# The last two casting loads of a Winograd convolution, each cut into two halves of 32 rows

## The chip, the cores and the metric

The kernel runs on one core of a Trainium2 chip. The metric is device time in microseconds (us), the median of the runs. The engines are named as in the profile: PE (TensorE: matmuls; PEld: its weight loads), DVE (VectorE), ACT (ScalarE), POOL (GpSimd) and SP (SyncE, which here only issues DMAs). All DMAs of the core run on 16 DMA engines.

## The reference

A 3x3 convolution with padding 1 over 16 images, 64 channels in, 128 out, 64x64 pixels, all in float32:

```python
batch, c_in, h, w, c_out = 16, 64, 64, 64, 128
x_pad = np.pad(x, ((0, 0), (0, 0), (1, 1), (1, 1)), mode='constant')
output = np.zeros((batch, c_out, h, w), dtype=np.float32)
for b in range(batch):
    for co in range(c_out):
        for ci in range(c_in):
            for kh in range(3):
                for kw in range(3):
                    output[b, co] += weight[co, ci, kh, kw] * x_pad[b, ci, kh:kh+h, kw:kw+w]
```

## The kernel before

The images are worked on in eight pairs `p`; two images of 64 channels fill the 128 partitions. A pair's input is one tile `xs[p]` of 64x64 float16 on each partition. The pool `xpool` has eight buffers, one for each pair, so no load waits for a buffer.

**How the input comes in.** Pairs 0 to 2 are loaded by SP as float32 (`x0`, `x1`, `x2`) and cast by ACT and POOL in pieces of 14 to 18 rows (L97 and L98). Pairs 3 to 7 are loaded by POOL with a DMA that casts from float32 to float16 on the way (`load`, L56 to L58), one DMA of 64 rows for a pair: 2 MB are read and 1 MB is written. POOL issues pairs 3 and 4 behind its casts of pair 0 (L107), and pairs 5, 6 and 7 one behind the other in pair 1's turn of the main loop (L132 to L134). No other DMA stands in POOL's queue.

**The scheme.** It is a Winograd form along the rows: two output rows 2j and 2j+1 share one product with the sum of the input rows 2j and 2j+1. `sums` (L62 to L67) forms these row sums `ss[p]`, for pair 0 on DVE and for all others on POOL, in two instructions of 16 sums (32 input rows) each, `lo` = 0 and 16. The pool `spool` has three buffers. The combined weights (`Wt`: G0, G21, G1, G01, G2) are made once at the start.

**The main loop** (L128) runs over the pairs. POOL first forms the sums of the next pair (L130, L131). Then come four blocks of 8 row pairs. A block has three groups of matmuls (L168): `U` from `ss` (6 matmuls), then `A` and `Bt` from `xs` (12 each, in pairs for the two images). ACT copies `U` out of PSUM (L182), DVE adds it to `A` (L190) and to `Bt` (L193) into the output tile `ot`. The rows of `xs` that a block reads follow from an offset: block 1 (sums 8 to 15) reads rows 15 to 31, and its last six matmuls (G2, offset 2) rows 18 to 32.

**The stores.** The first image of a pair is stored by SP, the second by ACT, each as one DMA of 2 MB, in halves of 1 MB for pair 7 and for the first image of pair 0. ACT's store is held back and issued in the next block's turn (L184). The output tiles have seven buffers, three of which first hold `x0` to `x2`.

**The order.** `keep` (L28) holds the marked instructions of one engine in the order in which the program has them: POOL's casts, sums and loads, ACT's copies and casts, ACT's stores. The framework sets the semaphores: each of POOL's DMAs reports its landing, and whoever reads the rows that it writes waits for that.

The lines of the change in their place:

Of the kernel before, what the change touches and what calls it, by code (L numbers as in the profile page):

```python
# [13 lines left out]
def kernel(  # L14
# [6 lines left out]
    nc = tc.nc  # L21
    B, CI, H, W = x.shape
# [5 lines left out]
    keep = tc.keep_in_program_order  # L28
    x_rows = x.rearrange("b c h w -> (b c) h w")
# [23 lines left out]

    xs = {p: xpool.tile([128, H, W], F16, tag="xs", name="xs") for p in range(3)}

    def load(p):  # L56
        xs[p] = xpool.tile([128, H, W], F16, tag="xs", name="xs")
        keep(nc.gpsimd.dma_start(xs[p], x_rows[128 * p : 128 * p + 128, :, :]))  # L58

    ss = {}  # L60

    def sums(eng, p, src, lo, n):  # L62
        if p not in ss:
            ss[p] = spool.tile([128, H // 2, W], F16, tag="ss", name="ss")
        v = src.rearrange("p (j i) c -> p j i c", i=2)
        keep(
            eng.tensor_add(  # L67
                ss[p][:, lo : lo + n, :], v[:, lo : lo + n, 0, :], v[:, lo : lo + n, 1, :]
            )
        )  # L70
# [26 lines left out]
    def cast(copy, p, src, lo, hi):  # L97
        keep(copy(xs[p][:, lo:hi, :], src[:, lo:hi, :]))  # L98
# [6 lines left out]
    cast(nc.gpsimd.tensor_copy, 0, x0, 34, 50)  # L105
    cast(nc.gpsimd.tensor_copy, 0, x0, 50, 64)
    for p in (3, 4):  # L107
        load(p)
    later = {
        (0, 0): [(0, x0, 18, 34)],  # L110
        (0, 2): [(1, x1, 0, 16), (1, x1, 16, 32)],
# [10 lines left out]
    def store(eng, p, b2, ot, lo, hi):  # L122
        return eng.dma_start(
            out_rows[2 * p + b2, :, lo:hi, :],
            ot.rearrange("p j i c -> p (j i) c")[:, lo:hi, :],
        )

    for p in range(NP):  # L128
        if p + 1 < NP:
            for lo in (0, 16):  # L130
                sums(nc.gpsimd, p + 1, raws.get(p + 1, xs[p + 1]), lo, 16)  # L131
                if (p, lo) == (1, 16):  # L132
                    for q in range(5, NP):
                        load(q)  # L134
        ots = [
            opool.tile([128, H // 2, 2, W], F32, tag="ot", name="ot") for _ in range(2)
        ]
        for blk in range(4):
            j0 = blk * RB

            def group(wi_rows):

                tiles = [
                    psum.tile([128, RB, W], F32, tag="acc", name="acc") for _ in range(2)
                ]
                n = 3 * len(wi_rows)
                i = 0
                for wi, off in wi_rows:
                    for kw in (1, 0, 2):
                        c_lo, c_hi = max(0, 1 - kw), min(W, W + 1 - kw)  # L150
                        for b2 in range(2):
                            p0 = 64 * b2
                            lo, hi = j0, j0 + RB
                            if off is None:
                                rhs = ss[p][p0 : p0 + 64, lo:hi, c_lo + kw - 1 : c_hi + kw - 1]
                            else:
                                while 2 * lo + off < 0:
                                    lo += 1
                                while 2 * (hi - 1) + off > H - 1:
                                    hi -= 1  # L160
                                first = 2 * lo + off
                                last = 2 * (hi - 1) + off
                                rhs = xs[p][
                                    p0 : p0 + 64,
                                    first : last + 1 : 2,
                                    c_lo + kw - 1 : c_hi + kw - 1,
                                ]
                            nc.tensor.matmul(  # L168
                                tiles[b2][:, lo - j0 : hi - j0, c_lo:c_hi],
                                Wt[p0 : p0 + 64, wi, kw, :],  # L170
                                rhs,
                                start=i == 0,
                                stop=i == n - 1,
                            )
                        i += 1
                return tiles

            U = group([(G1, None)])
            us = []
            for b2 in range(2):  # L180
                ut = upool.tile([128, RB, W], F32, tag="ut", name="ut")
                keep(nc.scalar.copy(ut, U[b2]))  # L182
                us.append(ut)
            while held and (p, blk) != (1, 0):  # L184
                keep(store(nc.scalar, *held.pop(0)))
            for piece in later.get((p, blk), ()):
                cast(nc.scalar.copy, *piece)
            A = group([(G21, 1), (G0, -1)])
            for b2 in range(2):
                nc.vector.tensor_add(ots[b2][:, j0 : j0 + RB, 0, :], A[b2], us[b2])  # L190
            Bt = group([(G01, 0), (G2, 2)])
            for b2 in range(2):
                nc.vector.tensor_add(ots[b2][:, j0 : j0 + RB, 1, :], Bt[b2], us[b2])  # L193
            if blk in cuts_of[p][0]:
                store(nc.sync, p, 0, ots[0], *cuts_of[p][0][blk])
            if blk in cuts_of[p][1]:
                held.append((p, 1, ots[1], *cuts_of[p][1][blk]))
# [32 lines left out]
```

## Time and profile before

| | us |
|---|---|
| median of 3 runs | 126.29 (126.21 to 126.46) |
| profiled execution, its own time | 126.58 |
| profiled execution, span from first to last instruction | 124.8 |
| PE busy | 107.6 (86%) |
| DVE busy | 84.5 (68%) |
| ACT busy | 46.5 (37%) |
| POOL busy | 37.5 (30%) |

The mean granted clock of PE is 0.971 of full speed, and is lower only in the last slices, when PE has ended. HBM is read for 17.07 MB and written with 33.55 MB by the instructions' account. The DMA part of the page counts a packet by the bytes that it writes, so a casting load of 2 MB in float32 shows as 1 MB. In that part q0 is POOL's queue, q1 SP's, q10 ACT's; q8 and q14 fetch instructions. The time of a queue is the sum of its packets' times as a share of 16 engines' span.

### The profile page before, as it was taken

To read this page: it belongs to the slowest core of one execution; us is meant where nothing else is said; L and a number is where in the kernel's file an instruction comes from. 1 tells how busy PE (TensorE), PEld (TensorE's weight loads), DVE (VectorE), ACT (ScalarE), POOL (GpSimd) and SP (SyncE) were. 2 spreads that over 40 slices of the span, in tenths; PEclk is the share of its full clock that TensorE was granted. 3 is DMA by queue.
4 is the path that set the end of the run, shared out by engine and by line. 5 is a ranking of instruction groups with operands and counts; after the bars stand their busy time and mean duration, and the time that the engine had idled before them with its cause. 6 is when DMAs were issued, how large, how long until landed. Compare 5 with 4: busy or idle time off the path is not lost.

```text
span 124.8 us, 2427 instructions
## 1 busy us (share of the span) xinstructions
PE 107.6 (86%) x984; PEld 50.2 (40%) x984; DVE 84.5 (68%) x135; ACT 46.5 (37%) x78; POOL 37.5 (30%) x28
## 2 busy tenths in 40 slices
PE   0598999999999999999999999999999999991000
PEld 0543444444444444444444444444444444440000
DVE  1009987878877887877777778777877787775000
ACT  4108649966663333333333333333333333330000
POOL 2209790899594003900066000930000000000000
PEclk9999999999999999999999999999999999999855
DMA  5999999999999999999999999999999999999991
GB/s 131 394 431 452 441 302 229 284 284 289 365 349 336 341 381 349 365 344 336 373 362 365 334 347 415 441 436 420 415 447 415 436 410 441 431 402 418 425 407 53
DMA packets 4042, 45.52 MB, mean 365 GB/s; under 512 B 448, under 2 KB 448, under 8 KB 576
## 3 DMA queue, kind: packets, MB, share of 16 engines
q1 hardware_dynamic: 2016, 23.36, 45.0%
q10 hardware_dynamic: 1296, 16.78, 31.7%
q0 software_dynamic: 720, 5.24, 20.5%
q8 instruction: 7, 0.11, 0.3%
q14 instruction: 3, 0.02, 0.0%
HBM read 17.07 MB, written 33.55 MB: 406 GB/s over the span
## 4 chain that ended last, share of the span: by engine, by line
PE 81%; DMA 6%; DVE 2%; issue 1%; DVEq 0%; SPq 0%
PE acc L168 81%; DMA x<-in_x_dram 6%; DVE ot L190 1%; DVE ss L67 1%; DVE ot L193 0%; DVEq L225 0%; SPq L41 0%; DVEq L190 0%
## 5 line engine op out<-in xcount | busy, mean ns | idle before, releaser
L168 PE MATMUL acc<-xs,Wt 64*128 64x504 f16 (+3 forms) x768 | 87.2, 373 | 0.0
L168 PEld LDWEIGHTS <-Wt 64*128 64x128 f16 x960 | 47.3, 94 | 56.2 <-issue 1.1
L182 ACT COPY ut<-acc 128x512 f32<-128x512 f32 x64 | 34.4, 589 | 56.9 <-issue 39.0
L190 DVE TENSOR_TENSOR ot<-acc,ut 128x512 f32<-128x512 f32 x64 | 41.2, 685 | 20.8 <-PE acc L168 18.4
L193 DVE TENSOR_TENSOR ot<-acc,ut 128x512 f32<-128x512 f32 x64 | 41.1, 683 | 0.0
L67 POOL TENSOR_TENSOR ss<-xs 128x1024 f16<-128x1024 f16 x10 | 21.1, 2127 | 32.6 <-DMA xs<-in_x_dram 20.5
L168 PE MATMUL acc<-ss,Wt 64*128 64x504 f16 (+1 forms) x192 | 26.1, 377 | 0.6 <-DVE ss L67 0.6
L98 ACT CAST xs<-x 128x1024 f16<-128x1024 f32 (+1 forms) x10 | 10.5, 1070 | 3.5 <-DMA x<-in_x_dram 3.5
L67 POOL TENSOR_TENSOR ss<-x 128x1024 f16<-128x1024 f32 x4 | 9.4, 2365 | 4.3 <-DMA x<-in_x_dram 4.3
L67 DVE TENSOR_TENSOR ss<-x 128x512 f16<-128x512 f32 x4 | 3.3, 867 | 7.8 <-DMA x<-in_x_dram 7.8
L85 PE MATMUL wp<-ident,w 128*64 128x128 f16 x18 | 1.3, 328 | 4.4 <-POOL w L52 4.4
L98 POOL CAST xs<-x 128x1024 f16<-128x1024 f32 (+1 forms) x2 | 3.0, 1519 | 4.7 <-DMA x<-in_x_dram 4.7
L91 PE MATMUL warm<-blank 128*128 128x400 f32 x6 | 3.6, 757 | 0.0
L85 PEld LDWEIGHTS <-w 128*64 128x64 f16 x18 | 1.1, 210 | 4.4 <-POOL w L52 4.4
L58 POOL DMA_DIRECT2D xs<-in_x_dram x5 | 2.9, 579 | 0.0
L91 PEld LDWEIGHTS warm<-blank 128*128 128x128 f32 x6 | 1.7, 304 | 1.4 <-issue 1.2
L92 ACT CAST Wt<-wp 128x384 f16<-128x384 f32 x1 | 0.5, 479 | 3.1 <-PE wp L85 3.1
L92 ACT ACT_TABLE_LOAD x1 | 1.3, 1283 | 0.7 <-PEq L214 0.7
L52 POOL CAST w<-w_raw 128x576 f16<-128x576 f32 x1 | 0.7, 662 | 2.4 <-DMA w_raw<-in_weight_dram 2.4
L88 DVE MEMSET blank<- 128x400 f32 x1 | 0.4, 392 | 0.9 <-PEq L214 0.9
L103 ACT CAST Wt<-wp 128x384 f16<-128x384 f32 x1 | 0.5, 478 | 0.5 <-DVE Wt L95 0.5
L94 DVE TENSOR_TENSOR Wt<-wp,Wt 128x384 f16<-128x384 f32 x1 | 0.6, 550 | 0.0
(8 smaller groups left out, 1.9 us busy)
## 6 DMA issues: line engine op xcount, KB each, us to landing
out_dram<-ot ACTq DMA_DIRECT2D x7, 2048.0 KB, 19.4
out_dram<-ot SPq DMA_DIRECT2D x6, 2048.0 KB, 19.1
x<-in_x_dram SPq DMA_DIRECT2D x3, 2048.0 KB, 12.3
xs<-in_x_dram POOLq DMA_DIRECT2D x5, 1024.0 KB, 21.7
out_dram<-ot SPq DMA_DIRECT2D x4, 1024.0 KB, 11.8
out_dram<-ot ACTq DMA_DIRECT2D x2, 1024.0 KB, 10.9
w_raw<-in_weight_dram SPq DMA_DIRECT2D x1, 288.0 KB, 2.9
```

The costliest lines, as they stand in the source:

```text
L52: keep(nc.gpsimd.tensor_copy(w16, w_raw))
L58: keep(nc.gpsimd.dma_start(xs[p], x_rows[128 * p : 128 * p + 128, :, :]))
L67: eng.tensor_add(ss[p][:, lo : lo + n, :], v[:, lo : lo + n, 0, :], v[:, lo : lo + n, 1, :])
L85: nc.tensor.matmul(wp[q : q + 64, k * CO : k * CO + CO], w16[:, t::9], ident)
L91: nc.tensor.matmul(warm[:, 0:400], blank[:, 0:128], blank)
L92: keep(nc.scalar.copy(wrow(G1), wps[1]))
L94: keep(nc.vector.tensor_sub(wrow(G21), wps[2], wrow(G1)))
L98: keep(copy(xs[p][:, lo:hi, :], src[:, lo:hi, :]))
L168: nc.tensor.matmul(tiles[b2][:, lo - j0 : hi - j0, c_lo:c_hi], Wt[p0 : p0 + 64, wi, kw, :], rhs, start=i == 0, stop=i == n - 1,)
L182: keep(nc.scalar.copy(ut, U[b2]))
L190: nc.vector.tensor_add(ots[b2][:, j0 : j0 + RB, 0, :], A[b2], us[b2])
L193: nc.vector.tensor_add(ots[b2][:, j0 : j0 + RB, 1, :], Bt[b2], us[b2])
```

## The change

`load` takes a number of rows and issues one DMA for each such part of the tile. Pairs 3, 4 and 5 come in one DMA of 64 rows as before; pairs 6 and 7 in two DMAs of 32 rows, one behind the other in POOL's queue. A half reads 8 KB that lie together from each of 128 channel planes (before: 16 KB) and writes 4 KB to each partition. POOL issues seven casting DMAs instead of five. Nothing else is edited.

```diff
-    def load(p):
+    def load(p, rows):
         xs[p] = xpool.tile([128, H, W], F16, tag="xs", name="xs")
-        keep(nc.gpsimd.dma_start(xs[p], x_rows[128 * p : 128 * p + 128, :, :]))
+        for lo in range(0, H, rows):
+            keep(
+                nc.gpsimd.dma_start(
+                    xs[p][:, lo : lo + rows, :],
+                    x_rows[128 * p : 128 * p + 128, lo : lo + rows, :],
+                )
+            )
...
     for p in (3, 4):
-        load(p)
+        load(p, H)
...
                 if (p, lo) == (1, 16):
                     for q in range(5, NP):
-                        load(q)
+                        load(q, H if q == 5 else H // 2)
```

## The prediction

> **What bounds the kernel now.** I read the page first: the engines' shares, the DMA row of the 40 slices, the queues and the chain.
>
> ```profile
> span 124.8 us, 2427 instructions
> PE 107.6 (86%) x984; PEld 50.2 (40%) x984; DVE 84.5 (68%) x135; ACT 46.5 (37%) x78; POOL 37.5 (30%) x28
> ...
> DMA  5999999999999999999999999999999999999991
> ...
> q1 hardware_dynamic: 2016, 23.36, 45.0%
> q10 hardware_dynamic: 1296, 16.78, 31.7%
> q0 software_dynamic: 720, 5.24, 20.5%
> ...
> PE 81%; DMA 6%; DVE 2%; issue 1%; DVEq 0%; SPq 0%
> ```
>
> At first sight this is a TensorE kernel: PE is the longest engine and carries 81% of the chain. But the chain follows instructions, and its last is the issue of a store near 114 us; the 11 us behind it, to 124.8, are transfers. And the DMA row shows 9 in every slice from the second to the last but one. The three data queues add up: 45.0 + 31.7 + 20.5 = 97.2% of the time of 16 DMA engines. q1 is SP's queue (the early plain loads and half of the stores), q10 ACT's (the other stores), q0 GpSimd's casting loads. Next I looked for gaps, in the table of stretches (columns: stretch, length, busy time of PE, PEld, DVE, ACT and POOL with their counts, clock, DMA share, GB/s):
>
> ```profile
> 40.00:55.00 15.00, 15.00 (x144) 6.91 (x140) 11.51 (x19) 5.03 (x10) 4.21 (x2) 1.00 1.01 354
> 78.00:100.00 22.00, 22.00 (x208) 10.17 (x206) 17.06 (x29) 7.52 (x14) 4.20 (x2) 1.00 1.01 432
> 100.00:112.00 12.00, 12.00 (x116) 5.53 (x112) 9.23 (x15) 4.29 (x8) 0.00 (x0) 1.00 1.00 419
> 112.00:122.50 10.50, 0.61 (x8) 0.10 (x2) 1.98 (x4) 0.00 (x0) 0.00 (x0) 0.76 0.93 393
> ```
>
> PE is full to 112, and the DMA share is 1.00 or 1.01 up to there too, with stores still to be drained. (The lower GB/s of 40 to 55 is bookkeeping: a casting load is counted by the bytes it writes, half of those it reads.) So two bounds run side by side, and the transfers end last. How far behind is PE's own path? The last two stores, one row of the timeline and one of the DMA view for 113 to 115, and the page's row of a small load (size, and us from issue to landing):
>
> ```profile
> 114.01 0.34 ACTq L123 DMA_DIRECT2D out_dram<-ot  x1
> ```
> ```profile
> out_dram<-ot SPq DMA_DIRECT2D x1, 1024.0 KB, 9.8
> ```
> ```profile
> w_raw<-in_weight_dram SPq DMA_DIRECT2D x1, 288.0 KB, 2.9
> ```
>
> The two last stores are 2 MB together: at the 393 GB/s of the last stretch 5.3 us. They land after 9.8, so 4.5 us are latency and waiting behind older stores. The small load bounds the latency: 288 KB at 432 GB/s are 0.7 us, so 2.2 of its 2.9 us are fixed. That leaves 2.3 us by which PE's last pair could be late before the end of the kernel moved. The end therefore moves by what the change adds to the work of the DMA engines, one for one, and by a late load only beyond that slack.
>
> **What the change adds for the DMA engines.** The counts in the page say how a transfer is cut. q0 has 720 packets in 5 loads, 144 each: 128, one per partition, and 16 small ones for completion. A half load therefore again has 144 packets, whose data packets read 8 KB instead of 16. Each engine gets 16 + 16 casting packets for pairs 6 and 7 instead of 8 + 8, the same bytes in all, and 2 more small ones. What does a packet cost? I asked the DMA view for stretches in which no completion packets fall. From 48.5 to 53.5 all three queues hold 16 KB packets, from 34.1 to 38.5 q1 holds 8 KB packets (the halves of pair 0's store), from 85 to 90 only 16 KB stores run, from 114.2 to 116 only 8 KB stores (columns: packets, MB, share of 16 engines):
>
> ```profile
> q0 software_dynamic: 44, 0.36, 34.3%
> q1 hardware_dynamic: 43, 0.70, 33.5%
> q10 hardware_dynamic: 43, 0.70, 32.8%
> ```
> ```profile
> q10 hardware_dynamic: 47, 0.77, 40.8%
> q0 software_dynamic: 45, 0.37, 39.9%
> q1 hardware_dynamic: 46, 0.38, 21.0%
> ```
> ```profile
> q1 hardware_dynamic: 66, 1.08, 50.6%
> ```
> ```profile
> q10 hardware_dynamic: 51, 0.42, 54.9%
> ```
>
> Share times length times 16, over packets, gives the time of one. First stretch: q0 34.3% of 80 us over 44 = 0.624 us, q1 0.623, q10 0.610. Second: q0 0.624, q10 0.611, and q1's 8 KB packet 0.321. Third: q1 0.613. Fourth: an 8 KB store 0.310. Two readings follow.
>
> First, the queues take turns packet by packet whatever the size: 44, 43, 43 where all are alike, and 47, 45, 46 where q1's are half as long. A round of three costs 0.624 + 0.623 + 0.610 = 1.857 us, and 8 rounds are one load: 14.9 us, against 14.3 to 14.6 between landings (below).
>
> Second, a packet of a store costs 0.01 us more when it stands behind a casting load: q1's is 0.623 against 0.610 to 0.613, and in the 8 KB size 0.321 against 0.310. The addition is the same for both sizes, so it belongs to the turn and not to the bytes.
>
> Now the sum. The change adds 8 rounds for each of two loads, 16 for each engine. If a half casting packet costs what q1's 8 KB packet costs in that mix, two halves are 0.642 where one whole was 0.624: +0.018. Each extra round also puts one more store packet behind a load: +0.012. That is 0.030 × 16 = 0.48 us. The times of packets overlap a little (their sum is 1.01 of the stretch), and each added border overlaps again: about 1% of 0.61 us, 0.006 × 16 = 0.1 us off. Left: 0.38 us, of which I take 0.36. Upper bound: no overlap and the completion packets, 0.5. Lower bound: the addition goes with bytes, not turns: 0. Below nothing: a half is exactly half of a plain 16 KB store, 0.306, and carries no turn at all: 16 × (0.612 − 0.624) = −0.2, and −0.3 with the overlap. I take the upper part because the row of q1's 8 KB packets, in the same mix, shows the turn paid in full by a half-sized packet.
>
> **What the change moves.** With smaller packets the loads get a smaller share of each round, so they land later. Rows: GpSimd's timeline, then PE's for the last pairs.
>
> ```profile
> 9.11 2.99 POOL L98 CAST xs<-x 128x1024 f16<-128x1024 f32 x2 [4.75 <-DMA x<-in_x_dram]
> ...
> 26.93 1.63 POOL L58 DMA_DIRECT2D xs<-in_x_dram  x3
> 28.56 4.23 POOL L67 TENSOR_TENSOR ss<-xs 128x1024 f16<-128x1024 f16 x2
> 34.54 4.21 POOL L67 TENSOR_TENSOR ss<-xs 128x1024 f16<-128x1024 f16 x2 [1.75 <-PE acc L168]
> 48.80 4.21 POOL L67 TENSOR_TENSOR ss<-xs 128x1024 f16<-128x1024 f16 x2 [10.05 <-DMA xs<-in_x_dram]
> 63.38 4.21 POOL L67 TENSOR_TENSOR ss<-xs 128x1024 f16<-128x1024 f16 x2 [10.37 <-PE acc L168]
> 77.98 4.21 POOL L67 TENSOR_TENSOR ss<-xs 128x1024 f16<-128x1024 f16 x2 [10.40 <-DMA xs<-in_x_dram]
> ```
> ```profile
> 86.83 0.81 PE L168 MATMUL acc<-ss,Wt 64*128 64x512 f16 x6
> ```
> ```profile
> 99.64 0.81 PE L168 MATMUL acc<-ss,Wt 64*128 64x512 f16 x6
> ...
> 103.44 2.76 PE L168 MATMUL acc<-xs,Wt 64*128 64x512 f16 x24
> ...
> 106.04 0.81 PE L168 MATMUL acc<-ss,Wt 64*128 64x512 f16 x6
> ```
>
> The sums of pairs 5, 6 and 7 start as their loads land, at 48.8, 63.4 and 78.0 (63.38 names PE, but the even step of 14.6 says that it is the load). A round now costs 0.321 + 0.623 + 0.610 = 1.554 us, 16 rounds 24.9. Pair 6's halves land near 61.2 and 73.7, pair 7's near 86.1 and 98.6, as long as both store queues stay filled; if one runs dry, sooner. Pair 6 is used by PE from 86.83: 13 us spare. Pair 7's first half feeds the sum of output blocks 0 and 1 (86.1 + 2.1 = 88.2, needed at 99.64). Its second half is read first by block 1's last six matmuls (row 32), about 2 us into the 24 that start at 103.44, and by the second sum, which takes 2.1 us and is needed at 106.04: so it must land by 103.9, and has 5.3 us to spare. That PE waits for rows and not for a whole tile shows at the start:
>
> ```profile
> L168 PE MATMUL acc<-xs,Wt x768: 349/377/378, 10.5 to 112.3; 64*128 64x504 f16 x112, 64*128 64x512 f16 x64, 64*128 64x441 f16 x16
> ```
>
> It reads pair 0 from 10.5, while GpSimd casts other rows of it until 12.1. So the new waits cost PE nothing here; without that cover, each us beyond 103.9 delays PE by one, and the end only beyond the 2.3 us of slack.
>
> What the loads lose, the stores gain: between 48.8 and 98.6 they move earlier, and what was left of loads comes later. The engines are busy either way, so this is an exchange and changes no sum; no compute engine waits for a store's buffer, since PE is full from 12 to 112.
>
> GpSimd issues two more DMAs. The three at 26.93 took 1.63 us, 0.54 each, so pair 3's sums, behind them in the queue, start 1.1 us later: at 29.7 instead of 28.56, and end near 33.9. Pair 4's start when its load lands at 34.54 anyway, and PE wants pair 3's near 48 (four pairs before 99.64 at 12.8 each). Nothing else is queued there. SP's and ACT's queues get no instruction.
>
> **Forecast.** 0.36 us on the DMA engines. The profiled execution took 126.58 us, 1.8 around its span; the median of the runs is 126.29, and I put the sum on that: 126.65. This is +0.29%, little beyond the 0.2% (0.25 us) that a measurement of this kernel can tell from none.
>
> **Rivals.**
> (A) The addition goes with the time that reading and writing are mixed, not with the turns: then twice the turns with half the reading cost nothing, 126.3. For it: only 0.01 us per packet separates the two. Against it: the row of 8 KB packets.
> (B) Faster. Half packets interrupt the stores for so short a time that the casting packet's excess over a store's (0.624 against 0.611) goes altogether, and with the smaller share of reads the store behind it pays none: −0.3 us by the lower bound above, 126.0. It decides if a half casting packet shows under 0.306 us. For it: nothing here shows an 8 KB casting packet. Against it: q1's 0.321.
> (C) Pair 7's second half lands after 103.9, because a half casting packet costs much more than half or the turns are not even. To move the end by 1 us it has to land at 107.2, 3.3 beyond 103.9, which is 29.2 us a load instead of 24.9. That gives 127.65. Against it: the even counts.
> (D) Each DMA has a fixed cost that holds the engines. The small load above has 2.2 us beside its bytes. If two more DMAs held all engines for that, 4.4 us would be added: 130.7. Against it: loads that are queued behind each other land 14.6 us apart, no more than their 8 rounds, so the fixed part of one lies beside packets of others. The Trainium skill, "DMA: Bandwidth & Descriptors", speaks against this change: its section "Anatomy of one DMA — SWDGE (gpsimd) path" gives each such DMA about 2.0 us beside its bytes, and "Rules for kernel authors" wants 1 MiB or more in one. By that page two more would make 130.3, an estimate; the trace does show the 2 us as a latency, but not as time of the engines.
>
> **Chances.** Forecast 0.52, A 0.20, B 0.20, C 0.04, D 0.04. Of the forecast's 0.52, some 0.08 lie under 0.25 us. Slower: 0.44 + 0.08 = 0.52; same: 0.20 + 0.08 = 0.28; faster 0.20. The range takes in B with 0.1 us of scatter, 125.9, and the upper bound with part of C, 127.1; D and the rest of C stay out.
>
> **What would show it.** Right: q0 with 1008 packets; from 50 to 95 even counts of packets in the three queues with q0's at 0.32 us and q1's still at 0.62; the last sums on GpSimd at about 86 and 98.6; PE without a new wait; DMA busy to the end. Wrong: a q0 packet under 0.31 us (A or B), a wait of PE near 99 to 106 (C), gaps in the DMA row (D), or a load share that is not one packet in three.

## The result, and the profile after

The change makes the kernel faster by 0.2%: 126.09 us (125.89 to 126.62) against 126.34 us (126.17 to 126.66), ratio 0.998 with an interval of 0.9972 to 0.9987. That is 0.25 us the other way from the forecast of +0.36.

The profiled execution of the changed kernel took 126.62 us, the slowest of its runs, with a span of 124.8. It shows the steps, but not the gain. First the page (queues: packets, MB, share of 16 engines):

```profile
span 124.8 us, 2430 instructions
...
DMA  5899999999999999999999999999999999999991
...
q1 hardware_dynamic: 2016, 23.36, 45.0%
q10 hardware_dynamic: 1296, 16.78, 31.7%
q0 software_dynamic: 1008, 5.24, 20.8%
```

q0 has 1008 packets instead of 720, and its share went from 20.5% to 20.8%: 0.3% of 124.8 us is 0.37 us more for every DMA engine. The other queues' shares stand. So the added work is there, in about the forecast size. Next the DMA view of the changed kernel, from 48 to 95 (completion packets are counted with the others) and from 62 to 64.5, where no completion packets fall:

```profile
q10 hardware_dynamic: 552, 8.00, 40.2%
q1 hardware_dynamic: 541, 7.82, 39.7%
q0 software_dynamic: 552, 2.04, 21.4%
```
```profile
q1 hardware_dynamic: 26, 0.43, 40.6%
q10 hardware_dynamic: 22, 0.36, 33.6%
q0 software_dynamic: 28, 0.11, 22.5%
```

The turns are nearly even, packet by packet: 552, 541, 552, or 488, 477 and 498 without the completion packets. In the short stretch a half casting packet costs 22.5% of 40 us over 28 = 0.321 us, q1's store behind it 0.625, q10's 0.611. GpSimd's timeline shows the landings of the four halves, and the waits of PE:

```profile
61.66 2.12 POOL L73 TENSOR_TENSOR ss<-xs 128x1024 f16<-128x1024 f16 x1 [8.06 <-DMA xs<-in_x_dram]
73.69 2.12 POOL L73 TENSOR_TENSOR ss<-xs 128x1024 f16<-128x1024 f16 x1 [9.91 <-DMA xs<-in_x_dram]
86.04 2.13 POOL L73 TENSOR_TENSOR ss<-xs 128x1024 f16<-128x1024 f16 x1 [10.23 <-DMA xs<-in_x_dram]
98.21 2.12 POOL L73 TENSOR_TENSOR ss<-xs 128x1024 f16<-128x1024 f16 x1 [10.04 <-DMA xs<-in_x_dram]
```
```profile
PE wp L91 <- POOL w L52: 4.3, 1, 4.3
```

Forecast were 61.2, 73.7, 86.1 and 98.6; PE has no wait but the one at the start. Every moved step is where it was expected, and yet the time goes down. Something that the sum does not hold must have become smaller by 0.25 + 0.37 = 0.6 us.

**Where it hides.** The views give means over 16 engines. The trace also holds each packet. Of the profile before, these are the store packets that start between 84.5 and 89.2 and took over 0.63 us, without the instruction fetch near 87.7 and the store behind it:

```
start us   84.540 85.194 85.844 86.474 87.114 87.764 88.413 89.062
queue         q10     q1    q10     q1    q10     q1    q10     q1
took us     0.658  0.653  0.634  0.644  0.653  0.653  0.653  0.644
```

Each starts where the one before ends, within 0.004 us (84.540 + 0.658 = 85.198): this is one DMA engine, working through both queues. From 80 to 100, 491 of 525 store packets took exactly 0.611 us and 33, one in 16, from 0.613 to 0.675. The DMA view shows one such packet too, for 85.19 to 85.20 (408.1% of 16 times 0.01 us is 0.653 us):

```profile
q1 hardware_dynamic: 1, 0.02, 408.1%
```

In the changed kernel, 902 of the 923 store packets from 50 to 95, where casting loads stand between them, took exactly 0.611 or 0.624: there no engine is slow. So behind the last load one engine of 16 needs on average 0.04 us more for each packet and falls behind; with a casting load in the round it does not. In the profile of before there are 58 such packets (0.626 to 0.675 us), nearly all on this engine, 2.16 us over 0.611 in sum; in that of the change, whose loads end at 97.8 instead of 77.5, 31 with 1.15 us. This engine gains 1.0 us and loses about 0.4 by turns. A store has landed when the last of its 16 engines is done.

### The profile page after: what moved, and what is told of

Its sections match the earlier page's. It is cut to its first block, busy times and chain, and to the rows that moved or that the text cites. A ratio compares the mean times of both kernels' runs of the same rounds, so it can differ in the third digit from the quotient of the medians.

```text
span 124.8 us, 2430 instructions
## 1 busy us (share of the span) xinstructions
PE 108.0 (86%) x984; PEld 49.8 (40%) x984; DVE 84.5 (68%) x135; ACT 46.5 (37%) x78; POOL 38.6 (31%) x30
## 3 DMA queue, kind: packets, MB, share of 16 engines
q0 software_dynamic: 1008, 5.24, 20.8%
## 4 chain that ended last, share of the span: by engine, by line
PE 86%; DMA 2%; DVE 1%; issue 1%; POOL 1%; DVEq 0%
PE acc L174 81%; PE warm L97 3%; DMA w_raw<-in_weight_dram 2%; PE wp L91 1%; DVE ot L196 1%; POOL w L52 1%; DVEq L231 0%; DVE ot L199 0%; DVEq L196 0%
## 5 line engine op out<-in xcount | busy, mean ns | idle before, releaser
L196 DVE TENSOR_TENSOR ot<-acc,ut 128x512 f32<-128x512 f32 x64 | 41.2, 685 | 20.8 <-PE acc L174 18.4
L97 PE MATMUL warm<-blank 128*128 128x400 f32 x6 | 4.2, 864 | 0.0
L60 POOL DMA_DIRECT2D xs<-in_x_dram x7 | 3.9, 574 | 0.0
```

The lines of the kernel that those rows point to most:

```text
L60: nc.gpsimd.dma_start(xs[p][:, lo : lo + rows, :], x_rows[128 * p : 128 * p + 128, lo : lo + rows, :],)
L97: nc.tensor.matmul(warm[:, 0:400], blank[:, 0:128], blank)
```

## The experiments

Each kernel was timed beside the kernel before. Ratios are to that, with 95% intervals.

**The same program, and the change once more.** `null` has whole loads through the changed function, `again` is the change.

```diff
-                        load(q, H if q == 5 else H // 2)
+                        load(q, H)
```

> All three late loads whole again through the changed function: the program of before. Every theory: the time of before, ratio 1.000 within 0.001. If it differs from before by as much as the change did (0.2%), the measured gain of the change is no effect of the loads at all.

Measured: 126.28, ratio 0.9994 (0.997 to 1.0017).

> The change once more, for a second measurement and a second profile. Theory 1 (the gain is real and lies in the end of the kernel): ratio 0.998, and a profile of an execution near the median shows the last transfer ended earlier than in the profile of before, by 0.2 to 0.3 us, with the 16 DMA engines ending closer together. Theory 2 (chance of the comparison): ratio 1.000 or above.

Measured: 126.15, ratio 0.9978 (0.9961 to 0.9995). The gain is real. This profiled execution took 126.09, near the median, and shows the end. The table of stretches for 122.5 to 123 and 123 to 123.5 (DMA share and GB/s are the last two columns; one 8 KB packet in half a us is 0.04), of before and then of this run:

```profile
122.50:123.00 0.50, 0.00 (x0) 0.00 (x0) 0.00 (x0) 0.00 (x0) 0.00 (x0) 0.50 0.08 33
123.00:123.50 0.50, 0.00 (x0) 0.00 (x0) 0.00 (x0) 0.00 (x0) 0.00 (x0) 0.50 0.04 16
```
```profile
122.50:123.00 0.50, 0.00 (x0) 0.00 (x0) 0.00 (x0) 0.00 (x0) 0.00 (x0) 0.50 0.16 66
123.00:123.50 0.50, 0.00 (x0) 0.00 (x0) 0.00 (x0) 0.00 (x0) 0.00 (x0) 0.50 0.00 0
```

Before, three packets start after 122.5, the last of them alone behind 123; in this run four start after 122.5 and none behind 123. The packet records agree: the last packet ends at 123.35 before and at 123.02 here, while the mean of the 16 engines' ends is 122.07 and 122.14. The mean hardly moved, and the last engine is earlier. But the profile of before is of an execution of 126.58 us, 0.24 above its median, and overstates the step. The profile of `null`, the same program as before in an execution of 126.17 us, has for the same stretches:

```profile
122.50:123.00 0.50, 0.00 (x0) 0.00 (x0) 0.00 (x0) 0.00 (x0) 0.00 (x0) 0.50 0.12 49
123.00:123.50 0.50, 0.00 (x0) 0.00 (x0) 0.00 (x0) 0.00 (x0) 0.00 (x0) 0.50 0.00 0
```

Its last packet ends at 123.09, with a mean of 122.15. Against this one the change ends only 0.07 us earlier, as its execution is 0.08 us shorter. Two profiles do not show where the 0.25 us between the medians lie.

**Which load is cut.** Pair 7 alone (`h7`), pairs 5 and 6 (`h56`), pair 5 alone (`h5`):

```diff
-                        load(q, H if q == 5 else H // 2)
+                        load(q, H // 2 if q == 7 else H)    # h7
+                        load(q, H if q == 7 else H // 2)    # h56
+                        load(q, H // 2 if q == 5 else H)    # h5
```

> Only pair 7's load in halves. The loads then end near 88 instead of 78 (before) and 98 (the change). Theory 1a (the gain comes from a load still in the queue near 98, so that the store queues do not run dry at 101 when pair 6's stores are issued): no gain, ratio 1.000 to 1.001. Theory 1b (each load with half packets gains by its share of the rounds): half of the gain, ratio 0.999. The turns alone (my forecast): 1.001.

Measured: 126.03, ratio 0.9974 (0.9959 to 0.999). Half the cut gains about as much as all of it, so theory 1a does not hold, as the gain needs no load in the queue at 98, and theory 1b's 0.999 lies at the edge of the interval. That sent me to the single packets.

> Pairs 5 and 6 in halves, pair 7 whole. As many extra turns as in the change, at an earlier time; the last load again lands near 98, but pair 7's rows then come all at once, so its first sum is ready near 100 and PE may wait up to 1 us at 99.6. Theory 1a: the gain of the change, 0.998. Theory 1b: the same, 0.998. The turns alone: 1.003. If PE's wait reaches the end: above 1.003.

Measured: ratio 0.9999 (0.9973 to 1.0024), median 126.53 with wide scatter. Its three fastest runs, 125.85 to 125.89, lie under the fastest of before, 126.16, but that is a hint only: undecided. PE did not wait; pair 7's load landed near 95.

> Only pair 5's load in halves, pairs 6 and 7 whole: the same extra turns as with pair 7 alone, at an earlier time; loads end near 88. Theory 2: when only 16 KB store packets run, one of the 16 DMA engines needs 0.64 to 0.66 us a packet where the others need 0.61 (48 such packets between 76 and 112 in the profile of before, 24 in that of the change); the end waits for the slowest engine, and a casting load in the round spares it. Then what counts is when the loads end: as with pair 7 alone, 0.997 to 0.998, some 31 slow packets. Rival (something of pair 7's own halves, for example its earlier first sum): 1.000.

Measured: 126.15, ratio 0.9988 (0.9971 to 1.0006), the loads ending at 86.0. The sign is that of theory 2, but the size is half and the interval holds 1, so it does not rule out that pair 7's cut is better. Nor did the slow packets fall as expected: 67 in this profile, since some of other engines lie in the same range.

**A later load without more turns.** `late7` issues pair 7's whole load behind pair 6's sums.

```diff
-                    for q in range(5, NP):
+                    for q in range(5, NP - 1):
                         load(q)
+                if (p, lo) == (5, 16):
+                    load(NP - 1)
```

> Whole loads as before, but pair 7's is issued only behind pair 6's sums, near 67.6 instead of 28.6. No extra turns. The loads end near 82 instead of 78, but the store queues are alone from 63 to 68, so the time in which only 16 KB stores run stays the same. Theory 2: 48 slow packets as before, some of them near 63 to 68, ratio 0.999 to 1.001. Rival (a load in the queue as late as possible is what gains): 0.999 or below.

Measured: 126.38, ratio 1.0 (0.9988 to 1.0012), 53 slow packets with 2.03 us, some of them from 62 to 72, where the loads paused. The last load ended at 87.4, as late as with pair 7 in halves, and gained nothing. A late load alone is not it; the time with stores alone is what stayed the same.

**The size of the store packets.** In `s8` the stores of pairs 3 to 6 go as two DMAs of 32 rows each at the same place; `s8_after` has the same on top of the change.

```diff
+    two = {3: (0, 32, 32, 64)}
+    cuts_of = [c if p < 3 or p == NP - 1 else (two, two) for p, c in enumerate(cuts_of)]
...
-            if blk in cuts_of[p][0]:
-                store(nc.sync, p, 0, ots[0], *cuts_of[p][0][blk])
+            rows = cuts_of[p][0].get(blk, ())
+            for i in range(0, len(rows), 2):
+                store(nc.sync, p, 0, ots[0], *rows[i : i + 2])
```

> Loads as before; the stores of pairs 3 to 6 go as two DMAs of 32 rows each, issued where the whole one was, so that the stretch without loads moves 8 KB packets instead of 16 KB ones. In the profile of before the 8 KB stores behind 112 show hardly a slow packet. Theory 2: the slow engine is gone or nearly so, the last transfers of the 16 engines end closer together, ratio 0.995 to 0.998. Rival (the turns between loads and stores, not the store packets, make the gain): 1.000, or above by the added packets, 0.1 us.

Measured: 126.96, ratio 1.0044 (1.0029 to 1.0059): slower, and theory 2 as I had put it is wrong. The slow engine does not need 16 KB packets. From 78 to 100, 1071 of 1139 packets took exactly 0.309 us, and 67, again about one in 16, 0.328 on average.

> The same cut of the stores on top of the change. Theory 2: the change now has nothing left to spare and only its extra turns remain, so this is slower than the cut of the stores alone by 0.2 to 0.4 us (0.002 to 0.003). Rival (independent gains): faster than the cut of the stores alone by 0.002.

Measured: 126.36, ratio 1.0004 (0.9991 to 1.0017). I expected the change to cost 0.2 to 0.4 us on top of `s8`; it gained 0.6. With the slow engine still there this is what the later end of the loads should do (75.8 in `s8`, 85.5 here). Theory 3: one engine falls behind while only stores run, whatever their packets' size; casting loads in the round spare it; each extra turn costs all engines 0.02 us.

**The opposite dose.** `s8_mid` leaves the loads whole and cuts the stores of pairs 1 and 2, which run beside them:

```diff
+    cuts_of = [(two, two) if p in (1, 2) else c for p, c in enumerate(cuts_of)]
```

> The opposite dose: loads whole, but the stores of pairs 1 and 2 cut in two DMAs of 32 rows, which run between 40 and 70 beside the loads. Half-sized store packets give the loads the larger share there, so they end sooner (near 70) and the stretch with stores alone grows from 35 to 42 us. Theory 3: more slow packets than before (55 to 60 of 16 KB), and slower, ratio 1.001 to 1.004. Rival (only the cut of loads does anything): 1.000 to 1.001 by the added packets.

Measured: 127.36, ratio 1.0061 (1.0035 to 1.0087), the last load ending at 66.0, 62 slow packets with 2.3 us. More than expected. The page and the end, as above:

```profile
span 125.5 us, 2437 instructions
...
q1 hardware_dynamic: 2304, 23.36, 44.8%
q10 hardware_dynamic: 1584, 16.78, 31.6%
q0 software_dynamic: 720, 5.24, 20.4%
```
```profile
122.50:123.00 0.50, 0.00 (x0) 0.00 (x0) 0.00 (x0) 0.00 (x0) 0.00 (x0) 0.50 0.12 49
123.00:123.50 0.50, 0.00 (x0) 0.00 (x0) 0.00 (x0) 0.00 (x0) 0.00 (x0) 0.50 0.08 33
```

The queues took 96.8% of 125.5 us, 121.5 us, against 97.2% of 124.8, 121.3, before. The mean work is the same within 0.2 us, and the mean of the engines' ends is 122.17 (before 122.07), but the last packet ends at 123.81 instead of 123.35. The loss lies in the slowest engine. For the store that ends near 102, the packet records tell which that is: its completion packet, directly behind a slow packet, comes 2.01 us after the first engine's, and no engine is later.

**More of the change, and the best one again.**

```diff
-                        load(q, H if q == 5 else H // 2)
+                        load(q, H // 2)    # h567
```

> Pairs 5, 6 and 7 in halves. Loads end near 107.5, so hardly a slow packet (under 10). But pair 7's second half is needed by 103.9: PE waits 3 to 4 us there, 2.3 us of which the end can bear. Theory 3 with this wait: 127.0 to 127.6, ratio 1.005 to 1.010, PE's wait named as one for the load or the sums. If the slack is larger than I reckoned, or only the slow engine counts: 0.996 to 1.000.

Measured: 126.46, ratio 0.9983 (0.995 to 1.0015). The slow packets were 30 instead of under 10. The wait of PE did not come: the last half landed at 103.8, because the halves did not come evenly (pair 6's first landed 12.4 us after the half before it, its second only 10.4 after that). The likely reason is a store queue that ran dry for a while, as stores were served faster than PE makes them; the sum had both queues filled throughout. So this run says nothing on the price of a late load. It lies between the change and before, without a decision.

> Pair 7's load alone in halves, a second time: the version with the lowest time so far. Theory 3 (one DMA engine falls behind while only stores run, whatever the size of their packets, and a casting load in the round spares it; extra turns cost all engines about 0.02 us each): loads end near 88, some 30 slow 16 KB packets, half the extra turns of the change, ratio 0.997 to 0.998, at or a little below the change.

Measured: 125.93, ratio 0.9944 (0.9908 to 0.998; the runs of before that it was timed beside scattered up to 128.85). The loads ended at 87.9, but this profile has 49 slow packets instead of some 30, with 1.67 us. Both measurements of pair 7 alone are below 1 by more than their intervals: medians 126.03 and 125.93 against 126.09 and 126.15 for the change. It beats the kernel before; that it beats the change by some 0.1 us is likely, not shown, as the two were timed side by side only once. In the profile of `h7` no data packet starts after 122.5.

**All in one table.** Slow packets are 16 KB store packets of 0.626 to 0.675 us between 58 and 112.5; their excess is over 0.611. A packet starts some 0.004 us before the end of the one before it on its engine, so the records can be strung into 16 chains, and the slow packets that follow one another lie on one of them. The table has the end of this engine, the end of the last of the other fifteen, and the time of the profiled execution, all in us.

| kernel | last load ends | slow packets, excess us | slow engine ends | last other ends | execution | ratio |
|---|---|---|---|---|---|---|
| stores of pairs 1 and 2 cut | 66.0 | 62, 2.3 | 123.81 | 122.82 | 127.25 | 1.0061 |
| stores of pairs 3 to 6 cut | 75.8 | 8 KB packets | 123.93 | 123.05 | 127.12 | 1.0044 |
| the same on top of the change | 85.5 | 8 KB packets | 123.05 | 123.18 | 126.36 | 1.0004 |
| before | 77.5 | 58, 2.16 | 123.35 | 122.99 | 126.58 | 1 |
| the same program | 78.4 | 57, 2.06 | 122.98 | 123.09 | 126.17 | 0.9994 |
| pair 7 later, whole | 87.4, with a pause | 53, 2.03 | 122.98 | 123.00 | 126.18 | 1.0 |
| pair 5 in halves | 86.0 | 67, 2.2 | 122.77 | 123.13 | 126.21 | 0.9988 |
| pair 7 in halves | 87.3 | 40, 1.45 | 122.62 | 122.78 | 125.88 | 0.9974 |
| pair 7 in halves, second time | 87.9 | 49, 1.67 | 122.69 | 122.84 | 125.92 | 0.9944 |
| pairs 5 and 6 in halves | 94.7 | 39, 1.39 | 122.55 | 123.04 | 126.16 | 0.9999 |
| the change, second time | 97.2 | 29, 1.04 | 122.41 | 123.02 | 126.09 | 0.9978 |
| the change, first time | 97.8 | 31, 1.15 | 122.36 | 123.51 | 126.62 | 0.998 |
| pairs 5, 6 and 7 in halves | 103.3 | 30, 1.09 | 122.28 | 123.13 | 126.38 | 0.9983 |

With the stores behind the loads whole, the slow engine ends earlier as the loads end later, from 123.81 to 122.28; the row of the pause stands with the same program. The two kernels with 8 KB stores make the same step, from 123.93 to 123.05. In three rows it ends last, by 0.99, 0.88 and 0.36 us: the two slower kernels and before. In all others another engine is last. So the change can gain only as far as the slow engine was the last, and from there on more cuts only add turns to the others. That would explain why half the cut does as well as all of it.

Who the others are shows in the second profile of the change: the six engines that served one of q8's instruction fetches behind 30 us end at 122.66 to 123.02, and eight of the rest at 121.35 to 121.91. On the engines with a fetch the price of the turns shows: in `null` five of the six ended at 122.37 to 122.41, some 0.5 us earlier, and one was the last with 123.09. The first profile of the change shows that the gain is not in every execution: its slow engine was done at 122.36, but one with a fetch at 102.1 ended at 123.51.

**When the engine is slow.** In three traces it turns slow 1.2 to 1.8 us behind its own last load: from 81.4 to 82.6 with pair 5 in halves, from 85.8 to 87.6 with pair 7, from 92.7 to 94.5 in the second profile of the change. And it stops near 114: from 114.5 on stores still run alone, and 390 of 391 data packets of that profile took 0.309. In it PE's last matmul ends near 112.5 and DVE's last addition near 113.8. So stores alone are not the whole condition, and by `s8` the packets' size is not the other part; whether the work of the compute engines is, no run tests.

## Why the prediction was wrong

**The bound was right:** transfers end last, PE has slack, and the DMA row shows no gap before the end.

**The price of a turn was right.** A half casting packet costs 0.321 us, the store behind it 0.625. q0's share rose by 0.37 us, where the sum had 0.29 for q0, 0.19 for the stores behind it and 0.1 off for the overlap, 0.38 in all; the engines with a fetch that can be compared ended some 0.5 us later. The mean of the 16 ends rose by less, from 122.07 and 122.15 to 122.14 and 122.25: in the two profiles without the cut, four or five engines that were ahead show a packet of 0.7 to 1.37 us near 101.5, and in the two of the change only one does, with 0.79. The landings came within 0.5 us, POOL's later sums and the second waits cost nothing.

**The step that failed** is the sentence "The end therefore moves by what the change adds to the work of the DMA engines, one for one". It takes 16 engines for one. The end belongs to the last of them, and one had a term of its own: 2.16 us of excess behind the last load, of which the change took away 1.0. It ended at 123.35 and 122.98 in the two profiles of the program before and at 122.36 and 122.41 in those of the change; the last of the others ended at 122.99 and 123.09, and at 123.02 and 123.51. The row to see it in was quoted: q1's 0.613 us from 85 to 90, where the other stretches had 0.610 and 0.611. I took it for the base of a packet. It was a mean of fifteen engines at 0.611 and one at 0.65. The second place was "What the loads lose, the stores gain ... this is an exchange and changes no sum". True for the sum; but the time from the last load to 112 changed from about 35 us to 14, and that had a price.

**Rival B** came near with 126.0, by luck: its reason did not occur, as a half packet shows 0.321 us, over its mark of 0.306. **A** asked for turns without cost, and q0's share speaks against it. **C** did not come up: the second half landed at 98.2, and even with three pairs in halves at 103.8. **D** is excluded: two more DMAs, and no 4.4 us. The Trainium skill ("DMA: Bandwidth & Descriptors", "Rules for kernel authors") wants 1 MiB or more in one DMA for the highest bandwidth. A half load reads 1 MiB and writes half of that, so these runs do not test that rule; they show only that the halves, with the other queues filled, cost their turns and no more.

What is shown: the slow engine, in which stretches it is slow, that it is the last one in the slower kernels and in one of the two profiles of the program before, and that its end moves with the end of the loads. That it makes the 0.25 us is argued from that: in the other profile of that program it was 0.11 us short of last, only the profiled executions have records of packets, and no run could take the slow engine away and leave the rest. Why this engine is slow there, and why a casting load spares it, stays open, and so does whether a plain load would do the same; that was not tried.

## What to carry to other kernels

A transfer ends with its slowest DMA engine, so a sum over mean shares says when the engines are done on average, not when the kernel ends. Before costing a change of transfers, look at how far apart the 16 completion packets of one transfer lie, and whether all packets of a kind took the same time; a mean that is 0.002 us off its neighbours can be one engine in 16 with 0.04 us on each packet. Here, spreading the loads over more of the time in which only stores would run was worth more than the turns that it added, but only as far as the slow engine was the last.

## What was not expected of the hardware

- With only stores in the queues and PE and DVE still at work, one DMA engine of 16 took 0.63 to 0.66 us for a 16 KB packet instead of 0.611, and 0.328 on average for an 8 KB packet instead of 0.309. With casting loads between them all took the same, and so they did behind 114.5, with PE and DVE done (0.309). The Trainium skill, "DMA: Bandwidth & Descriptors", section "Latency and other measured facts", says that engines 7 and 15 are usually slower and guesses at the descriptor rings of GpSimd's transfers. The records do not name the engine, but the guess does not fit this one: it is slow when GpSimd has no transfer in flight.
- An instruction fetch (q8, 7 of them, 16 KB each) takes 0.88 to 0.97 us of one DMA engine, and the 16 KB store packet that follows on the same engine mostly 0.95 to 1.02 instead of 0.611. Together that sets one engine back by about 1.3 us.
- A casting packet and the store behind it each cost 0.013 us more than a store among stores, in the 16 KB and in the 8 KB size alike.
